# Attention slots of a decoder trunk: stick-breaking mask by GpSimd selects, fp32r carry, earlier differential combination, and two output pieces per PSUM bank

## The chip, the cores and the metric

The kernel runs on one core of a Trainium2 chip. The metric is the device time of one execution in microseconds; lower is better. The kernel before takes 606.7 us (median of three runs, 604.87 to 609.16).

Names used below: PE is TensorE (matmul), PEld its weight loads, DVE is VectorE, ACT is ScalarE, POOL is GpSimd, SP is the queue that issues most transfers.

## The reference, cut to what matters

One layer on x of 256 rows by 1024 columns, float32: a SwiGLU block, a mixer, a SwiGLU block, each followed by a residual add and a layer norm. The mixer runs three causal attentions in parallel (6 heads of 64 each) and merges them with sigmoid gates. The change touches two of them and the way the outputs of all three are stored.

```python
def stick_breaking_attention(q, k, v):
    z = jnp.einsum('bhcd,bhsd->bhcs', qc, k) * scale
    log_1m = jnp.where(before, jax.nn.log_sigmoid(-z), 0.0)      # before: key s < query t
    tail = lax.cumsum(log_1m, axis=3, reverse=True) - log_1m
    w = jnp.where(before, jnp.exp(jax.nn.log_sigmoid(z) + tail), 0.0)
    return einsum(w, v)

def diff_attention(q, k, v, slopes, lam, subln_g, lambda_init):
    p = jax.nn.softmax(s, axis=-1)            # two maps per head
    w = p[:, :, 0] - lam * p[:, :, 1]
    o = einsum(w, v)                          # then a headwise RMS norm
```

MoBA attention, with blocks as long as the sequence, is here a causal softmax with a distance bias.

## The kernel before, in words

The program is one stream per engine, written out by hand in Python; nothing reorders it (`manual_schedule`). Its backbone is weight matmuls. Every float32 weight chunk of 128 by 1024 is loaded by SP, split by ACT (high part `h`, L106) and DVE (rest `l`, L107) into two fp32r tiles, and used in three fp32r products (`nat_mm`, L381, or `trn_mm`, L389), all accumulated in PSUM tiles named `acc` (4 banks). `Weights.pump` splits ahead: each `W.done` frees a chunk and puts the next splits into ACT's and DVE's queues at that place.

The mixer walks the list `MIX` (L44): query and key projections of a pair of heads (`project`, L772), gates (`gates`, L807), branch outputs (`branch`, L829). Between them stand the attention slots. `project` queues a `slot` (L759) by `pe.later`: a model of PE's time (`Pe`, L144) runs a queued job before the matmul at which it falls due. A slot starts one new pair of heads and moves every pair under way on by one stage. So one slot is a burst of small float32 matmuls on PE, in the middle of weight matmuls, in the order of `KINDS` (L612).

There are nine pairs: three stick-breaking (S1 to S3), then three differential (D1 to D3), then three MoBA (M1 to M3), and eleven slots:

| slot | stages on PE, in order |
|---|---|
| 1 | S1 mask, S1 scores |
| 2 | S1 sums, S2 mask, S1 carry, S2 scores |
| 3 | S2 sums, S3 mask, S2 carry, S1 values, S3 scores |
| 4 | S3 sums, S3 carry, S2 values, D1 scores |
| 5 | D1 turn, S3 values, D2 scores |
| 6 | D1 pv, D2 turn, D3 scores |
| 7 | D1 turn_o, D2 pv, D3 turn, M1 scores |
| 8 | D2 turn_o, D3 pv, M1 turn, M2 scores |
| 9 | D3 turn_o, M1 values, M2 turn, M3 scores |
| 10, 11 | M2 values, M3 turn; M3 values |

Small products live in PSUM tiles `att` (4 banks of 512 columns). Per stage:

- Stick-breaking (`stick_pair`, L710). `mask` writes a mask of 0 and -1e30 into the two score banks by a matmul with the identity (`identr`, `maskr`); the scores are added on top (`start`). ACT and DVE make softplus of the scores (L726 to L729), ACT copies its high part into `ln_g` and DVE writes the rest into `ln_b` (`act_split`, L233). One slot later `sums` adds reverse cumulative sums (matmuls with the triangle `trir`), and `carry` adds the second block's total to the first by a float32 matmul with `mones`. ACT takes the exponential (L745) into tile `eT`. Another slot later `values_T` multiplies by V.
- Differential (`diff_pair`, L641). DVE adds the distance bias and finds row limits (L582), ACT exponentiates (L585). `combine` (L657) forms one map from two per head, in DVE's queue at 5.0 and 7.0 us of modelled PE time after the scores (`D_C0`, `D_C1`). A slot later `turn` transposes (ACT copies out, L593), then `pv` multiplies by V, DVE normalises out of PSUM (L680), and `turn_o` transposes the result.
- MoBA (`moba_pair`, L614). As a softmax; `norm` (L628) scales rows on DVE 4.0 us of modelled time after the scores (`M_N`), then `turn` and `values_T`.
- Storing. `values_T`, `pv` and `turn_o` take one `att` bank each. `act_split` empties that of `values_T` and `turn_o` into `oT`: ACT first (L234), DVE after it (L235); both read the bank.

Of the kernel before, what the change touches and what calls it, by code (L numbers as in the profile page):

```python
# [10 lines left out]
F32 = mybir.dt.float32  # L11
F32R = mybir.dt.float32r
AF = mybir.ActivationFunctionType
ALU = mybir.AluOpType
# [37 lines left out]
T_X1 = 5.9  # L52
T_M = 3.4
N_T = 3.0
M_N = 4.0
D_C0 = 5.0
D_C1 = 7.0
D_S = 2.5
E_BUFS = 6

# [128 lines left out]
def trunk(ctx: ExitStack, tc: tile.TileContext, start_d, x_d, ln_g, ln_b, gu_d, gun_d, down_d, v_d, qk_d, gate_d,  # L189
# [78 lines left out]

    with ExitStack() as es:
        st = es.enter_context(tc.tile_pool(name="start2", bufs=1))  # L270
        identr = const.tile([P, P], F32R, name="identr")
        nc.gpsimd.tensor_copy(identr, ident)
        mhalf = const.tile([P, 8], F32, name="mhalf")
        nc.gpsimd.memset(mhalf, -0.5)
        base = const.tile([P, BW], F32, name="base")
        iv = st.tile([P, BW], mybir.dt.int32, name="iv")
        nc.gpsimd.iota(iv[:, 0:P], pattern=[[1, P]], base=0, channel_multiplier=-1)
        nc.gpsimd.iota(iv[:, P:BW], pattern=[[1, S]], base=-P, channel_multiplier=-1)
        nc.gpsimd.tensor_copy(base, iv)
        nc.gpsimd.affine_select(base[:, 0:P], base[:, 0:P], pattern=[[-1, P]], compare_op=ALU.is_ge, fill=NEG,  # L280
                                base=0, channel_multiplier=1)
        nc.gpsimd.affine_select(base[:, P:BW], base[:, P:BW], pattern=[[-1, S]], compare_op=ALU.is_ge, fill=NEG,
                                base=P, channel_multiplier=1)
        maskf = st.tile([P, BW], F32, name="maskf")
        nc.gpsimd.memset(maskf, 0.0)
        for c in (0, S):
            nc.gpsimd.affine_select(maskf[:, c:c + P], maskf[:, c:c + P], pattern=[[1, P]], compare_op=ALU.is_gt,
                                    fill=NEG, base=0, channel_multiplier=-1)
        maskr = const.tile([P, BW], F32R, name="maskr")
        nc.gpsimd.tensor_copy(maskr, maskf)  # L290
        tri = st.tile([P, P], F32, name="tri")
        nc.gpsimd.memset(tri, -1.0)
        nc.gpsimd.affine_select(tri, tri, pattern=[[-1, P]], compare_op=ALU.is_ge, fill=0.0, base=0,
                                channel_multiplier=1)
        trir = const.tile([P, P], F32R, name="trir")
        nc.gpsimd.tensor_copy(trir, tri)
        mones = const.tile([P, P], F32, name="mones")
        nc.gpsimd.memset(mones, -1.0)
        qsc = const.tile([P, 9], F32, name="qsc")
        for b in range(3):  # L300
            for p in range(NP):
                for r in range(2):
                    h = 2 * p + r
                    v = 0.125 / SLOPES[2 * h] if b == 0 else 32.0 ** -0.5 / SLOPES[2 * h + 1] if b == 1 else 0.125
                    nc.gpsimd.memset(qsc[r * 64:(r + 1) * 64, b * NP + p:b * NP + p + 1], v)
# [221 lines left out]
    with ExitStack() as es:  # L527
# [32 lines left out]
        def scores(maps, qT, kT, row_q):  # L560


            st, mv = (qT, kT) if row_q else (kT, qT)
            first = row_q
            for kind in range(2):
                for r0, n, ps in maps:
                    r, tp = slice(r0, r0 + n), (r0, 0)
                    if row_q and kind == 0:
                        out, a, b_ = ps[:, 0:P], slice(0, P), slice(0, P)
                    elif row_q:  # L570
                        out, a, b_ = ps[:, P:BW], slice(P, S), slice(0, S)
                    elif kind == 0:
                        out, a, b_ = ps[:, 0:S], slice(0, P), slice(0, S)
                    else:
                        out, a, b_ = ps[:, S:BW], slice(P, S), slice(P, S)
                    pe.mm(out, st[r, a], mv[r, b_], first, first, tile_position=tp, share=len(maps),
                          skip_group_check=not row_q)

        def exp_rows(ps, slope, e, nmx, sm):
# [8 lines left out]
        def turn_rows(e):  # L588
# [4 lines left out]
            nc.scalar.activation(eT, ps[:, :BW], AF.Copy)  # L593
            return eT

        def values_T(b, p, eTs):

            po = att.tile([P, 512], F32, name="att")
            for kt, cs, ws in ((0, slice(0, S), slice(0, S)), (1, slice(P, S), slice(S, BW))):
                for r in range(2):  # L600
                    pe.mm(po[r * HD:(r + 1) * HD, cs], V[:, kt, vcol(b, 2 * p + r)], eTs[r][:, ws], kt == 0, kt == 1,
                          tile_position=(0, r * 64), share=2, skip_group_check=True)
            act_split(oT[b][:, p, 0:S], oT[b][:, p, S:2 * S], po[:, 0:S])
            pairs_done[b] += 1

        exps = [0]
# [2 lines left out]

        KINDS = ("sums", "mask", "carry", "turn_o", "pv", "turn", "valT", "scores")  # L612

        def moba_pair(p, qT, kT):  # L614
            sm = small.tile([P, 2, 2], F32, name="sm")
# [25 lines left out]
        def diff_pair(p, qT, kT):  # L641
# [4 lines left out]
            def start():  # L646
# [10 lines left out]
                def combine(r):  # L657
# [4 lines left out]
                    for t, cs in enumerate((slice(0, P), slice(P, BW))):  # L662
                        nc.vector.scalar_tensor_tensor(e0[:, cs], e1[:, cs], c[:, t:t + 1], e0[:, cs],  # L663
                                                       op0=ALU.mult, op1=ALU.add)
                pe.later(D_C0, lambda: combine(0))
                pe.later(D_C1, lambda: combine(1))

            def pv():
                ps = att.tile([P, 512], F32, name="att")
                for r in range(2):  # L670
                    vc, eT = vcol(1, 2 * p + r), eTs[r]
                    o0, o1 = ps[:, r * HD:(r + 1) * HD], ps[:, P + r * HD:P + (r + 1) * HD]
# [5 lines left out]
                o = ep.tile([P, S], F32, name="o", bufs=1)  # L678
                o4 = o.rearrange("p (t r c) -> p t r c", t=2, r=2)
                nc.vector.tensor_tensor(  # L680
                    o4, ps[:, 0:S].rearrange("p (t r c) -> p t r c", t=2, r=2),
                    rs.rearrange("p r t -> p t r").unsqueeze(3).to_broadcast([P, 2, 2, HD]), op=ALU.mult)
                sq = ep.tile([P, S], F32, name="s1", bufs=3)
                nc.vector.tensor_tensor(sq, o, o, op=ALU.mult)
# [11 lines left out]
                pe.later(D_S, scale)  # L696

            def turn_o():
                ps = att.tile([P, 512], F32, name="att")
                for t in range(2):  # L700
                    pe.tr(ps[:, t * P:(t + 1) * P], os_[0][:, t * P:(t + 1) * P], ident)
                act_split(oT[1][:, p, 0:S], oT[1][:, p, S:2 * S], ps[:, 0:S])
                pairs_done[1] += 1

            return [{"scores": start},
# [2 lines left out]
                    {"turn_o": turn_o}]  # L708

        def stick_pair(p, qT, kT):  # L710
            zs, sps, wts, split = [], [], [], []

            def mask():
                zs.extend(att.tile([P, 512], F32, name="att") for _ in range(2))
                for ps in zs:
                    pe.mm(ps[:, 0:BW], identr, maskr, True, False, skip_group_check=True)

            def start():
                scores([(r * 64, 64, zs[r]) for r in range(2)], qT, kT, False)
                sh = lnp.tile([P, D], F32R, name="ln_g")  # L720
                sl = lnp.tile([P, D], F32R, name="ln_b")
                split.extend((sh, sl))
                for r in range(2):
                    ps = zs[r]
                    a = ep.tile([P, BW], F32, name="e")
                    nc.scalar.activation(a, ps[:, 0:BW], AF.Abs)  # L726
                    nc.scalar.activation(a, a, AF.Exp, scale=-1.0)
                    nc.scalar.activation(a, a, AF.Ln, bias=1.0)
                    nc.vector.scalar_tensor_tensor(a, ps[:, 0:BW], 0.0, a, op0=ALU.max, op1=ALU.add)  # L729
                    sps.append(a)  # L730
                    cs = slice(r * BW, (r + 1) * BW)
                    act_split(sh[:, cs], sl[:, cs], a)

            def sums():
                for r in range(2):
                    for part in split:
                        pe.mm(zs[r][:, 0:BW], trir, part[:, r * BW:(r + 1) * BW], False, False,
                              skip_group_check=True)

            def carry():  # L740
                for r in range(2):
                    pe.mm(zs[r][:, P:S], mones, sps[r][:, S:BW], False, True, skip_group_check=True)
                for r in range(2):
                    w = ep.tile([P, BW], F32, name="eT", bufs=4)
                    nc.scalar.activation(w, zs[r][:, 0:BW], AF.Exp)  # L745
                    wts.append(w)
                exps[0] -= 1

            return [{"mask": mask, "scores": start},
                    {"sums": sums, "carry": carry},  # L750
                    {"valT": lambda: values_T(2, p, wts)}]

        attend = (moba_pair, diff_pair, stick_pair)
# [5 lines left out]
        def slot(new=None):  # L759
            if new is not None:  # L760
                under_way.append(new)
                begun[0] += 1
            now = [pair.pop(0) for pair in under_way]
            for kind in KINDS:
                for stage in now:
                    if kind in stage:
                        stage[kind]()
            under_way[:] = [pair for pair in under_way if pair]
            if begun[0] == 3 * NP and under_way:
                pe.later(PACE, slot)  # L770
# [159 lines left out]
```

## Time and profile before

| what | us |
|---|---|
| device time, median of three runs (lowest, highest) | 606.7 (604.87, 609.16) |
| the profiled execution | 606.8 |
| its span, first to last instruction | 605.1 |
| PE busy in the span | 593.8 (98%) |
| DVE, ACT, POOL busy | 407.5, 328.5, 26.9 |
| mean granted TensorE clock, of full speed | 0.995 |

The profiled execution lasted 1.7 us longer than its span; that is what lies around the first and the last instruction. The eleven slots lie between 222 and 357 us of the span. A timeline row gives start, duration, engine, line, operation, written tile, read tiles, shape and count; in square brackets stands how long the engine had been idle and what ended it. Rows merge neighbours of one kind, and a merged row lasts to the end of its last instruction. Float32 matmuls appear as two records each.

### The profile page before, as it was taken

Reading aid. Unit: us, or ns where it says so; the run is one execution under the profiler, and the core shown is the slowest. Engines: PE = TensorE matmul, PEld = TensorE weight load, DVE = VectorE, ACT = ScalarE, POOL = GpSimd, SP = SyncE. Lnnn points to the kernel's source line nnn. Section 1 sums busy time; section 2 is a strip of 40 time slices with the busy share of each in tenths; the row PEclk is TensorE's granted clock in tenths of the full one; section 3 lists DMA queues with packets and bytes.
Section 4 is the critical chain, followed back from the end, with each engine's and each line's share of the span. In section 5 each row is a group of like instructions: output and inputs, shape, how many; then the busy total and the mean of one; then the engine's idle time right before and its main releaser. Section 6 shows DMA issues by size and latency. Waiting matters only on the chain.

```text
span 605.1 us, 8603 instructions
## 1 busy us (share of the span) xinstructions
PE 593.8 (98%) x3168; PEld 506.5 (84%) x3168; DVE 407.5 (67%) x665; ACT 328.5 (54%) x561; POOL 26.9 (4%) x63
## 2 busy tenths in 40 slices
PE   8999999999999999999999999999999999999995
PEld 7888888888889988888787878888888888888884
DVE  5879767674438665577778585889857667664217
ACT  6869656653312777576556654544655655653100
POOL 1610000000001000000001000001000000000001
PEclk9999999999999999999999999999999999999998
DMA  8898755566531784444447447346965565565001
GB/s 315 289 369 307 288 181 193 186 207 202 156 104 62 249 316 166 140 147 133 144 136 221 162 140 247 117 172 228 340 194 185 185 198 173 187 192 190 1 0 70
DMA packets 32539, 113.35 MB, mean 187 GB/s; under 512 B 3681, under 2 KB 4449, under 8 KB 32497
## 3 DMA queue, kind: packets, MB, share of 16 engines
q1 hardware_dynamic: 30816, 106.97, 52.4%
q0 software_dynamic: 1680, 5.83, 2.8%
q8 instruction: 25, 0.41, 0.3%
q14 instruction: 18, 0.14, 0.1%
HBM read 111.74 MB, written 1.05 MB: 186 GB/s over the span
## 4 chain that ended last, share of the span: by engine, by line
PE 95%; DVE 2%; ACT 1%; DMA 1%; issue 1%; SPq 0%; DVEq 0%; ACTq 0%
PE acc L180 89%; PE att L180 4%; PE att L184 2%; DMA sraw<-start 1%; DVE w L107 1%; ACT e L585 1%; ACT w L106 0%; DVE e L663 0%; DVE x L356 0%; ACT eT L593 0%; SPq L244 0%; DVE x L352 0%; DVE w L235 0%; ACT w L234 0%; ACT eT L745 0%
## 5 line engine op out<-in xcount | busy, mean ns | idle before, releaser
L107 DVE TENSOR_TENSOR w<-raw,w 128x1024 fp32r<-128x1024 f32 (+1 forms) x166 | 197.6, 1206 | 75.1 <-ACT w L106 74.9
L180 PE MATMUL acc<-xT,w 128*128 128x512 f32 x1264 | 225.3, 338 | 0.0
L180 PEld LDWEIGHTS acc<-xT,w 128*128 128x128 f32 x1264 | 193.6, 188 | 28.6 <-issue 1.0
L106 ACT ACTIVATE w<-raw 128x1024 fp32r<-128x1024 f32 (+1 forms) x166 | 170.3, 1041 | 80.0 <-PE acc L180 66.4
L180 PE MATMUL acc<-w,xT 128*128 128x512 f32 (+1 forms) x576 | 129.2, 379 | 0.0
L180 PEld LDWEIGHTS acc<-w,xT 128*128 128x128 f32 x576 | 105.2, 188 | 18.0 <-issue 1.0
L180 PE MATMUL acc<-w,hT 128*128 128x512 f32 (+1 forms) x408 | 93.5, 383 | 0.0
L180 PEld LDWEIGHTS acc<-w,hT 128*128 128x128 f32 x408 | 74.9, 188 | 14.9
L459 ACT ACTIVATE lo<-acc 128x256 f32<-128x256 f32 x76 | 27.8, 375 | 58.2 <-PE acc L180 58.2
L461 DVE TENSOR_TENSOR gu<-acc,lo 128x256 f32<-128x256 f32 x76 | 31.2, 419 | 38.6 <-ACT lo L459 38.6
L107 DVE TENSOR_TENSOR wx<-raw,wx 128x1024 fp32r<-128x1024 f32 (+1 forms) x30 | 36.3, 1212 | 12.0 <-ACT wx L106 12.0
L180 PE MATMUL acc<-xT,wx 128*128 128x512 f32 x240 | 44.0, 338 | 0.0
L180 PEld LDWEIGHTS acc<-xT,wx 128*128 128x128 f32 x240 | 36.7, 188 | 5.4
L106 ACT ACTIVATE wx<-raw 128x1024 fp32r<-128x1024 f32 (+1 forms) x30 | 31.3, 1046 | 10.9 <-PE acc L180 10.4
L180 PE MATMUL acc<-wx,hT 128*128 128x512 f32 (+1 forms) x138 | 32.8, 380 | 0.0
L180 PEld LDWEIGHTS acc<-wx,hT 128*128 128x128 f32 x138 | 25.2, 188 | 4.9
L338 DVE SCALAR_TENSOR_TENSOR x<-x,acc 128x512 f32<-128x512 f32 x11 | 7.5, 682 | 28.0 <-PE acc L180 28.0
L180 PE MATMUL acc<-w,oT 128*128 128x512 f32 x108 | 26.0, 394 | 0.0
L347 POOL TENSOR_TENSOR rs<-rs,mhalf 128x1 f32<-128x1 f32 x6 | 5.9, 979 | 408.0 <-DVE rs L346 408.0
L234 ACT ACTIVATE hT<-gu 128x256 fp32r<-128x256 f32 x40 | 16.6, 415 | 13.1 <-DVE gu L466 12.1
L180 PEld LDWEIGHTS acc<-w,oT 128*128 128x128 f32 x108 | 20.0, 188 | 4.4 <-issue 0.3
L465 ACT ACTIVATE gu<-gu 128x256 f32<-128x256 f32 x40 | 16.4, 409 | 2.8 <-DVE gu L461 2.6
(135 smaller groups left out, 401.4 us busy)
## 6 DMA issues: line engine op xcount, KB each, us to landing
raw<-gu SPq DMA_DIRECT2D x76, 512.0 KB, 4.9
raw<-down SPq DMA_DIRECT2D x44, 512.0 KB, 4.1
raw<-gates SPq DMA_DIRECT2D x24, 512.0 KB, 4.4
raw<-qk SPq DMA_DIRECT2D x18, 512.0 KB, 4.5
raw<-v SPq DMA_DIRECT2D x12, 384.0 KB, 3.1
raw<-w_out SPq DMA_DIRECT2D x8, 512.0 KB, 4.3
raw<-gun SPq DMA_DIRECT2D x8, 512.0 KB, 4.6
sraw<-start SPq DMA_DIRECT2D x7, 384.0 KB, 6.4
```

The source lines that it names most:

```text
L106: self.nc.scalar.activation(h[:, :n], raw[:, :n], AF.Copy)
L107: self.nc.vector.tensor_tensor(l[:, :n], raw[:, :n], hv[:, :n], op=ALU.subtract)
L180: self.nc.tensor.matmul(out, lhsT=lhsT, rhs=rhs, start=start, stop=stop, **kw)
L184: self.nc.tensor.transpose(out, in_, ident)
L234: nc.scalar.activation(dst_h, src, AF.Copy)
L338: nc.vector.scalar_tensor_tensor(xs, xs, ALPHA, ps[:, 0:n], op0=ALU.mult, op1=ALU.add)
L347: nc.gpsimd.tensor_tensor(rs, rs, mhalf[:, 0:1], op=ALU.pow)
L459: nc.scalar.activation(lo, ps[:, S:2 * S], AF.Copy)
L461: nc.vector.tensor_tensor(v, ps[:, 0:S], lo, op=ALU.add)
L465: nc.scalar.activation(g, g, AF.Silu)
L585: nc.scalar.activation(e[:, cs], e[:, cs], AF.Exp, bias=nmx[:, t:t + 1], scale=-1.0, accum_out=sm[:, t:t + 1])
```

## The change

Four edits, all inside the slots:

1. The mask matmuls go. The first score matmul now opens the accumulation, and GpSimd zeroes the future with `affine_select` twice per head: on the softplus tile before it is split (`unseen(a)`), and on the exponential (`unseen(w)`).
2. The carry is done in fp32r, on the two parts (`ln_g`, `ln_b`) that the sums use, right after each head's sums; it was one float32 matmul per head. Each head's exponential follows its own carry.
3. `combine` of a differential pair is queued at once, behind its exponentials, and `M_N` falls from 4.0 to 2.0.
4. `half_bank` hands out halves of an `att` bank: within one slot the first two of `turn_o`, `pv` and `values_T` share a bank.

```diff
-M_N = 4.0
-D_C0 = 5.0
-D_C1 = 7.0
+M_N = 2.0
...
-        mones = const.tile([P, P], F32, name="mones")
+        mones = st.tile([P, P], F32, name="mones")
         nc.gpsimd.memset(mones, -1.0)
+        monesr = const.tile([P, P], F32R, name="monesr")
+        nc.gpsimd.tensor_copy(monesr, mones)
...
-                    pe.mm(out, st[r, a], mv[r, b_], first, first, tile_position=tp, share=len(maps),
+                    pe.mm(out, st[r, a], mv[r, b_], row_q or kind == 0, row_q, tile_position=tp, share=len(maps),
...
+        halves = []
+
+        def half_bank():
+
+            if not halves:
+                ps = att.tile([P, 512], F32, name="att")
+                halves.extend((ps[:, 0:S], ps[:, S:2 * S]))
+            return halves.pop(0)
+
         def values_T(b, p, eTs):
 
-            po = att.tile([P, 512], F32, name="att")
+            po = half_bank()
...
-        KINDS = ("sums", "mask", "carry", "turn_o", "pv", "turn", "valT", "scores")
+        KINDS = ("sums", "turn_o", "pv", "turn", "valT", "scores")
...
-                pe.later(D_C0, lambda: combine(0))
-                pe.later(D_C1, lambda: combine(1))
+                for r in range(2):
+                    combine(r)
 
             def pv():
-                ps = att.tile([P, 512], F32, name="att")
+                ps = half_bank()
...
             def turn_o():
-                ps = att.tile([P, 512], F32, name="att")
+                ps = half_bank()
...
-            def mask():
+            def unseen(a):
+
+                blocks = a.rearrange("p (n c) -> p n c", c=P)[:, 0:3:2, :]
+                nc.gpsimd.affine_select(blocks, blocks, pattern=[[0, 2], [1, P]], compare_op=ALU.is_gt, fill=0.0,
+                                        base=0, channel_multiplier=-1)
+
+            def start():
                 zs.extend(att.tile([P, 512], F32, name="att") for _ in range(2))
-                for ps in zs:
-                    pe.mm(ps[:, 0:BW], identr, maskr, True, False, skip_group_check=True)
-
-            def start():
...
-                    sps.append(a)
+                    unseen(a)
                     cs = slice(r * BW, (r + 1) * BW)
                     act_split(sh[:, cs], sl[:, cs], a)
...
-
-            def carry():
-                for r in range(2):
-                    pe.mm(zs[r][:, P:S], mones, sps[r][:, S:BW], False, True, skip_group_check=True)
-                for r in range(2):
+                    for n, part in enumerate(split):
+                        pe.mm(zs[r][:, P:S], monesr, part[:, r * BW + S:(r + 1) * BW], False, n == 1,
+                              skip_group_check=True)
                     w = ep.tile([P, BW], F32, name="eT", bufs=4)
                     nc.scalar.activation(w, zs[r][:, 0:BW], AF.Exp)
+                    unseen(w)
                     wts.append(w)
...
             now = [pair.pop(0) for pair in under_way]
+            halves.clear()
```

Three places show what moves. The first is PE in slot 7, with buffer numbers and the engines waited for. `ident,o` are the transposes of `turn_o` for D1, `V,eT` the matmuls of `pv` for D2, `ident,e` the transposes of `turn` for D3. Before:

```order
L184 MATMUL att_3066<-ident_117,o_2895 128x128 x2
L180 MATMUL att_3071<-V_1930,eT_2907 128x64 [waits Activation_49]
L180 MATMUL att_3071<-V_1930,eT_2907 128x64 x2
L180 MATMUL att_3071<-V_1930,eT_2913 128x64 x3
L184 MATMUL att_3088<-ident_117,e_2927 128x128 x3
```

and now:

```order
L182 MATMUL att_3068<-ident_117,o_2897 128x128 [waits Activation_49]
L182 MATMUL att_3068<-ident_117,o_2897 128x128
L178 MATMUL att_3068<-V_1920,eT_2909 128x64 [waits DVE_49]
L178 MATMUL att_3068<-V_1920,eT_2909 128x64 x2
L178 MATMUL att_3068<-V_1920,eT_2915 128x64 [waits Activation_49]
L178 MATMUL att_3068<-V_1920,eT_2915 128x64 x2
L182 MATMUL att_3089<-ident_117,e_2929 128x128 [waits PE_49]
```

`turn_o` and `pv` wrote two banks (att_3066, att_3071) and now write one (att_3068). The first matmul of `pv` waited for an ACT copy of the slot before and now waits for DVE: for the subtraction by which `act_split` empties the half that `turn_o` wrote. Slot 8 has the same rows, and in slot 9 the first `values_T` matmul of M1 waits so for D3's `turn_o`.

The second place is the row of DVE in which D2's maps are combined, from the last row limits of slot 5 on. `qT` and `kT` empty a projection, `w<-raw,w` are weight splits, the rows with `c` are `combine`. Before:

```order
L787 SCALAR_TENSOR_TENSOR qT<-acc,qsc,s_2812 128x256
L790 TENSOR_TENSOR kT<-acc,s_2833 128x256
L107 TENSOR_TENSOR w<-raw,w 128x1024 x2
L659 RECIPROCAL c<-smd 128x2
L660 SCALAR_TENSOR_TENSOR c<-smd,nlam,c 128x2
L663 SCALAR_TENSOR_TENSOR e<-e,c 128x128
L663 SCALAR_TENSOR_TENSOR e<-e,c 128x256
L107 TENSOR_TENSOR w<-raw,w 128x1024
L659 RECIPROCAL c<-smd 128x2
L660 SCALAR_TENSOR_TENSOR c<-smd,nlam,c 128x2
L663 SCALAR_TENSOR_TENSOR e<-e,c 128x128
L663 SCALAR_TENSOR_TENSOR e<-e,c 128x256
```

and now:

```order
L658 RECIPROCAL c<-smd 128x2
L659 SCALAR_TENSOR_TENSOR c<-smd,nlam,c 128x2
L662 SCALAR_TENSOR_TENSOR e<-e,c 128x128
L662 SCALAR_TENSOR_TENSOR e<-e,c 128x256
L658 RECIPROCAL c<-smd 128x2
L659 SCALAR_TENSOR_TENSOR c<-smd,nlam,c 128x2
L662 SCALAR_TENSOR_TENSOR e<-e,c 128x128
L662 SCALAR_TENSOR_TENSOR e<-e,c 128x256
L788 SCALAR_TENSOR_TENSOR qT<-acc,qsc,s_2824 128x256
L791 TENSOR_TENSOR kT<-acc,s_2845 128x256
L105 TENSOR_TENSOR w<-raw,w 128x1024 x3
```

Both combinations moved ahead of the projection's emptying and of three weight splits.

The third place is POOL from the first norm's powers to the end of the stick-breaking pairs; `e` is the softplus tile, `eT` the exponential, `bg` the gate bias. Now:

```order
L338 TENSOR_TENSOR rs<-rs,mhalf 128x1 x2
L715 AFFINE_SELECT e<-e 128x2x128 x2
L812 DMA bg<-b_gate 128x1024 x2
L715 AFFINE_SELECT eT<-eT 128x2x128 x2
L715 AFFINE_SELECT e<-e 128x2x128 x2
L715 AFFINE_SELECT eT<-eT 128x2x128 x2
L715 AFFINE_SELECT e<-e 128x2x128 x2
L715 AFFINE_SELECT eT<-eT 128x2x128 x2
```

Before, only the two powers and the two transfers of `bg` stood there; twelve selects are added, two of them ahead of `bg`.

## Rows read from the trace of the kernel before

**Rows 1.** The chain that ended last, by engine (page, part 4).
```profile
PE 95%; DVE 2%; ACT 1%; DMA 1%; issue 1%; SPq 0%; DVEq 0%; ACTq 0%
```
**Rows 2.** Waits of PE inside the mixer: line waited for, us in total, times, longest.
```profile
PE att L184 <- DVE e L663: 0.9, 1, 0.9
PE att L180 <- ACT eT L593: 0.5, 2, 0.3
PE att L180 <- ACT eT L745: 0.4, 1, 0.4
```
**Rows 3.** Timeline, PE in slot 2: mask, carry, scores.
```profile
234.03 0.51 PE L180 MATMUL att<-maskr,identr 128*128 128x384 f32 x2
...
234.38 0.61 PE L180 MATMUL att<-e,mones 128*128 128x128 f32 x4
...
234.92 0.92 PE L180 MATMUL att<-qT,kT 64*128 64x256 f32 x8
```
**Rows 4.** Timeline, PEld in slot 7: pv, six float32 matmuls of 64 columns.
```profile
306.60 1.42 PEld L180 LDWEIGHTS att<-V,eT 128*128 128x128 f32 x12
```
**Rows 5.** Timeline, POOL's selects at the start, and DVE beside them.
```profile
14.88 5.24 DVE L107 TENSOR_TENSOR w<-raw,w 128x1024 fp32r<-128x1024 f32 x4 [0.71 <-ACT w L106]
...
17.66 1.37 POOL L282 TENSOR_SCALAR_AFFINE_SELECT base<-base 128x256 f32<-128x256 f32 x1
...
21.30 0.29 POOL L293 TENSOR_SCALAR_AFFINE_SELECT tri<-tri 128x128 f32<-128x128 f32 x1
```
**Rows 6.** Timeline, S3: end of its split, and its first sum in slot 4.
```profile
257.48 0.56 DVE L235 TENSOR_TENSOR ln_b<-e,ln_g 128x384 fp32r<-128x384 f32 x1 [0.59 <-ACT ln_g L234]
...
260.02 0.35 PE L180 MATMUL att<-ln_g,trir 128*128 128x384 f32 x1
```
**Rows 7.** Gate bias: first use (timeline); its transfers, us to landing (page, part 6).
```profile
244.53 1.28 DVE L825 TENSOR_TENSOR G<-acc,bg 128x512 f32<-128x512 f32 x2
...
bg<-b_gate POOLq DMA_DIRECT2D x3, 512.0 KB, 8.4
```
**Rows 8.** Timeline, PEld in slots 6 and 5: turn, and what follows it.
```profile
289.72 0.37 PEld L184 LDWEIGHTS att<-ident,e 128*128 128x128 f32 x3
...
291.96 0.19 PEld L180 LDWEIGHTS acc<-kT,qT 32*128 32x128 f32 x2 [0.17 <-issue]
...
277.06 0.79 PEld L184 LDWEIGHTS att<-ident,e 128*128 128x128 f32 x6
...
278.02 0.63 PEld L180 LDWEIGHTS att<-eT,V 128*64 128x64 f32 x8 [0.17 <-issue]
```
**Rows 9.** Timeline, slot 7: pv on PE; DVE up to emptying turn_o's bank.
```profile
306.71 1.45 PE L180 MATMUL att<-V,eT 128*128 128x64 f32 x12
306.82 2.36 DVE L107 TENSOR_TENSOR w<-raw,w 128x1024 fp32r<-128x1024 f32 x2 [0.52 <-ACT w L106]
...
309.10 0.42 DVE L235 TENSOR_TENSOR oT<-att,oT 128x256 fp32r<-128x256 f32 x1
```
**Rows 10.** Timeline, slot 8: the same, with the MoBA scaling (L633) on DVE.
```profile
316.32 2.36 DVE L107 TENSOR_TENSOR w<-raw,w 128x1024 fp32r<-128x1024 f32 x2 [0.52 <-ACT w L106]
...
318.27 1.45 PE L180 MATMUL att<-V,eT 128*128 128x64 f32 x12
...
318.80 1.01 DVE L633 TENSOR_SCALAR e<-e,rsm 128x128 f32<-128x128 f32 x4
...
320.12 0.41 DVE L235 TENSOR_TENSOR oT<-att,oT 128x256 fp32r<-128x256 f32 x1
```
**Rows 11.** Timeline, slot 9: M1's values on PE; DVE empties turn_o's bank, then M1's.
```profile
330.86 0.87 PE L180 MATMUL att<-eT,V 128*64 128x256 f32 x8
...
332.09 0.75 DVE L235 TENSOR_TENSOR oT<-att,oT 128x256 fp32r<-128x256 f32 x2
```
**Rows 12.** Windows at the end: us, PE, PEld, DVE, ACT, POOL busy (x), PEclk, DMA, GB/s.
```profile
597.50:598.00 0.50, 0.26 (x3) 0.06 (x1) 0.20 (x1) 0.00 (x0) 0.00 (x0) 1.00 0.00 0
...
599.50:600.00 0.50, 0.00 (x0) 0.00 (x0) 0.50 (x2) 0.00 (x0) 0.50 (x1) 0.63 0.00 0
```

More of the change, by code (lines that the diff above doesn't have):

```diff
@@ L270, in trunk @@
         st = es.enter_context(tc.tile_pool(name="start2", bufs=1))
-        identr = const.tile([P, P], F32R, name="identr")
-        nc.gpsimd.tensor_copy(identr, ident)
         mhalf = const.tile([P, 8], F32, name="mhalf")
@@ L283, in trunk @@
                                 base=P, channel_multiplier=1)
[L284 to L290, printed above, removed]
         tri = st.tile([P, P], F32, name="tri")
@@ L563, in scores @@
             st, mv = (qT, kT) if row_q else (kT, qT)
-            first = row_q
             for kind in range(2):
@@ L602, in values_T @@
                           tile_position=(0, r * 64), share=2, skip_group_check=True)
-            act_split(oT[b][:, p, 0:S], oT[b][:, p, S:2 * S], po[:, 0:S])
+            act_split(oT[b][:, p, 0:S], oT[b][:, p, S:2 * S], po)
             pairs_done[b] += 1
@@ L680, in pv @@
                 nc.vector.tensor_tensor(
-                    o4, ps[:, 0:S].rearrange("p (t r c) -> p t r c", t=2, r=2),
+                    o4, ps.rearrange("p (t r c) -> p t r c", t=2, r=2),
                     rs.rearrange("p r t -> p t r").unsqueeze(3).to_broadcast([P, 2, 2, HD]), op=ALU.mult)
@@ L698, in turn_o @@
             def turn_o():
-                ps = att.tile([P, 512], F32, name="att")
+                ps = half_bank()
                 for t in range(2):
                     pe.tr(ps[:, t * P:(t + 1) * P], os_[0][:, t * P:(t + 1) * P], ident)
-                act_split(oT[1][:, p, 0:S], oT[1][:, p, S:2 * S], ps[:, 0:S])
+                act_split(oT[1][:, p, 0:S], oT[1][:, p, S:2 * S], ps)
                 pairs_done[1] += 1
@@ L710, in stick_pair @@
         def stick_pair(p, qT, kT):
-            zs, sps, wts, split = [], [], [], []
-            def mask():
+            zs, wts, split = [], [], []
+            def unseen(a):
[3 more added lines that the diff above has]
+            def start():
                 zs.extend(att.tile([P, 512], F32, name="att") for _ in range(2))
-                for ps in zs:
-                    pe.mm(ps[:, 0:BW], identr, maskr, True, False, skip_group_check=True)
-            def start():
                 scores([(r * 64, 64, zs[r]) for r in range(2)], qT, kT, False)
@@ L738, in sums @@
                               skip_group_check=True)
-            def carry():
-                for r in range(2):
-                    pe.mm(zs[r][:, P:S], mones, sps[r][:, S:BW], False, True, skip_group_check=True)
-                for r in range(2):
+                    for n, part in enumerate(split):
+                        pe.mm(zs[r][:, P:S], monesr, part[:, r * BW + S:(r + 1) * BW], False, n == 1,
+                              skip_group_check=True)
                     w = ep.tile([P, BW], F32, name="eT", bufs=4)
                     nc.scalar.activation(w, zs[r][:, 0:BW], AF.Exp)
+                    unseen(w)
                     wts.append(w)
                 exps[0] -= 1
-            return [{"mask": mask, "scores": start},
-                    {"sums": sums, "carry": carry},
+            return [{"scores": start},
+                    {"sums": sums},
                     {"valT": lambda: values_T(2, p, wts)}]
```

## Prediction, written before the changed kernel was run

> **What bounds the kernel now.** I read the chain of waits first. 95% of the span lies on PE, 1% each on ACT and on transfers and 2% on DVE [rows 1]. So an edit pays only by the PE time it takes out or the PE waits it ends, and it costs what it puts on PE, work or wait. Then I read the waits of PE inside the mixer: four, 1.8 us in all [rows 2]. One is for the combination (DVE, L663, slot 6), two are for an ACT copy of transposed rows (L593, slots 7 and 8), one is for an exponential (L745, slot 3). All four are waits for an operand or for an `att` bank, and the change goes for all of them. Last I read the timeline of the slots for what DVE and ACT do while PE is in a slot. There the change adds three waits, so most of the working below is about them.
>
> **Mask and carry on PE.** In slot 2 the mask matmuls start at 234.03, the carry at 234.38, the scores at 234.92 [rows 3]. So the mask takes 0.35 us of PE and the carry 0.54 us, per pair. Three masks go: 3 x 0.35 = 1.05 us gained. The carry becomes four fp32r matmuls of 128 columns per pair. No fp32r matmul that narrow is in the trace. The nearest row is `pv`, whose twelve records are narrower still (64 columns) and take 1.42 us, 0.118 us each [rows 4]: at that size the record, not its columns, sets the time. I take 4 x 0.118 = 0.47 us, a gain of 3 x (0.54 - 0.47) = 0.2 us. The two ends: if only columns counted, a third of the mask's 0.175 us, 0.058 us each, the gain is 3 x (0.54 - 0.23) = 0.9 us; if narrow fp32r ran no faster than a carry matmul of before, 0.54 / 2 = 0.27 us each, there is a loss of 3 x (1.08 - 0.54) = 1.6 us.
>
> **Selects on GpSimd.** Twelve, of 256 elements per partition each. At the start a select of 128 took 0.29 us while DVE's splits were over, and one of 256 took 1.37 us while four of them ran [rows 5]. I take 0.4 us, since the select on the softplus follows DVE's own last step and DVE's next one waits for the split behind it; the ends are 0.3 and 1.4. A new wait comes with it: ACT's copy of the high part now waits for POOL, and behind it in ACT's queue stand the next head's softplus, the copies of a projection and weight splits. That is about 0.9 us more per pair. The tightest pair is S3: its split ends at 257.48 + 0.56 = 258.04 and the first sum starts at 260.02 [rows 6], a cover of 1.98 us. So it is hidden, and at 1.4 us (2.8 in all) up to 0.8 us shows. PE waits nowhere in the mixer for a weight split [rows 2], so splits 0.9 us late cost nothing as long as that cover lasts. The selects on the exponentials have a whole slot until the values read them. The `bg` transfers move behind S1's first selects, so at the latest to slot 2, by when S1's split must be done: 234 us [rows 3]. Landing takes 8.4 us and the first use is at 244.53 [rows 7], so 2 us at least are left over: nothing.
>
> The Trainium skill (SBUF — State Buffer, "SBUF: two separate sides") says that GpSimd and a DVE instruction with two SBUF inputs lock each other out of a shared port pair for a whole instruction. The two selects of rows 5 fit it: 1.37 us beside such splits. By that rule a select costs at most one split more, which is the upper end already taken, and the sum stays as it is.
>
> **The exponential's bank (slot 3).** S1's values waited 0.4 us for a bank that S2's first exponential had to free [rows 2]. Without the early masks the values take a bank free since slot 2, and each exponential starts half a stage earlier. Gain 0.4 us.
>
> **Combination at once (slot 6).** Transposes took 289.72 to 291.96 there, 2.24 us; the same six took 277.06 to 278.02, 0.96 us, in slot 5, where nothing was waited for [rows 8]. Queued behind the exponentials, the maps are ready before slot 6 begins, so 1.28 us go. Late next is the bank that D3's scores take over from `pv`: DVE can normalise as soon as `pv` ends, while PE transposes, so nothing follows. The price is that DVE waits for ACT's eight exponentials with a projection's emptying and splits behind it. PE waits for none of these in the mixer [rows 2], so I count nothing; without that cover, the 1.28 us come back.
>
> **Two pieces per bank.** In slots 7 and 8 the scores waited twice, 0.5 us in all, for a bank that an ACT copy had to free [rows 2]; one bank less per slot ends that: gain 0.5 us. But the second piece now waits until DVE has emptied the first, and DVE has weight splits ahead of that. PE stands in order, so everything behind the first matmul of the second piece waits too: `pv`, `turn`, the scores, then the weight matmuls.
> - Slot 7: `pv` started at 306.71. DVE splits two chunks from 306.82 to 309.18, then empties `turn_o` from 309.10 to 309.52 [rows 9]. These follow the projection's end as before, and the combination moved away stood ahead of them. Loss 309.52 - 306.71 = 2.81 us.
> - Slot 8: `pv` started at 318.27, the emptying at 320.12. The smaller `M_N` takes the scaling, 1.01 us, out of DVE's way, to a place ahead of the splits that end at 318.68 [rows 10]. So 320.12 - 1.01 + 0.41 = 319.52. Loss 1.25 us; 2.26 us if the scaling were still in the way.
> - Slot 9: M1's values started at 330.86; DVE begins the two emptyings at 332.09 behind a split [rows 11], and the first ends 0.42 us later (its length in rows 9). Loss 332.51 - 330.86 = 1.65 us.
>
> Together 5.7 us. A piece alone in its bank (slots 3 to 6, 10, 11) pays nothing.
>
> The Trainium skill (PSUM — Partial Sum Buffer, "PSUM bank collisions raise a hardware error") says that TensorE must not write a bank in the partitions where another engine reads it, even in other columns. So halves of one bank can't be filled and emptied at once, and the wait is none that a finer bookkeeping of columns could drop; without the rule the 5.7 us would be 0. No run here shows the collision itself.
>
> **The sum.** Gains: 1.05 + 0.2 + 0.4 + 1.28 + 0.5 = 3.4 us. Losses: 5.7 us. Net 2.3 us more. The profiled execution took 606.8 us (605.1 span, 1.7 around it), 0.1 over the median, so I forecast 606.8 + 2.3 = 609.1 us, 0.4% slower. About 1%, 6 us, is what a measurement of this kernel can tell from no change, so this counts as the same. Its own range is 607 to 611.5: carry from +0.7 to -1.8 around my term, 1.0 us more in slot 8, 0.8 us for slow selects, 1 us less if ACT and DVE reach the emptying sooner.
>
> **Rivals.**
> - The gains alone: the three half-bank waits are short, because DVE comes to the emptying as soon as ACT has copied. The row of DVE speaks against it: two splits in slot 7, one in slot 9 stand ahead in program order, and each must wait for ACT. For it speaks only that splits have moved elsewhere on DVE. It decides if the three waits together are under 3.4 us. Time 606.8 - 3.4 = 603.4 us, faster. Chance 0.14.
> - The clock falls in slot 7. PE ended at about 597.8; the granted clock was 1.00 for nearly two us more, then in the window from 599.5 it was 0.63 on the way to the lower of its two levels, 1.2 GHz [rows 12]. A stop of 2.8 us in slot 7 is longer than that. Against it: no stop inside the mixer was over 0.9 us [rows 2], so no row shows a fall between bursts, nor how long a low stretch lasts. Each us at the lower level loses half a us. If it takes as long to rise as it took to fall, 1 us is lost; if it lasts to slot 8, 11 us on, 5.5 us. I take 1.5: 610.6 us, up to 614.6. Chance 0.25.
> - The selects are slow, 1.4 us each, and the carry as slow as before per matmul: 0.8 + 1.8 us more, 611.7 us. Speaking for it: the only select of that width took 1.37 us. Against: DVE is idle in that step. Chance 0.08.
>
> The Trainium skill (TensorE: Matmul & The Clock Gate, "Why this matters for your kernels") warns of idle gaps between bursts of matmuls, since the clock goes back to its lower level. The end of this trace agrees that it does.
>
> **How the numbers follow.** Forecast 0.53, gains alone 0.14, clock 0.25, slow selects and carry 0.08. The likeliest gives 609.1. The range takes in the gains alone at 603.4 and ends at 612.5, which leaves out the upper tail of the clock case. Faster by over 1% (under 600.7) would need all gains and more: 0.02. Slower by over 1% (over 612.8) is that tail and a little of the last case: 0.07. Within 1%: 0.91.
>
> **What would show it.** Right: three new waits of PE for DVE's emptying of `oT`, near 2.8, 1.25 and 1.65 us, the only long ones in the mixer; slot 6 without a wait for the combination; no row of `maskr`; narrow carry records near 0.12 us; selects near 0.4 us and no PE wait for `ln_g` or `ln_b`; granted clock 1.00 through slots 7 to 9. Wrong: PE waits under 3.4 us in all there (faster), a granted clock below 1.00 behind slot 7, or PE waiting for POOL or for a weight split (slower).

## The result, and the profile after

The changed kernel takes 610.3 us (median of 22 executions, 606.59 to 613.38), the kernel before, run beside it, 606.88 (22 executions). The ratio is 1.0052, with 95% interval 1.0037 to 1.0067: 3.2 us slower (2.2 to 4.1). The forecast was 2.3 us slower, 609.1.

The execution that was profiled took 606.59 us, the fastest of the 22, and 0.2 us less than the profiled one of before. So this trace alone doesn't show the loss. Rows of its chain of waits and of that of before show why: where the long run of weight matmuls starts, what follows slot 11, and the last block. Before:

```profile
17.86 168.10 PE acc L180 x892
...
356.99 27.92 PE acc L180 x122
...
439.29 158.49 PE acc L180 x839
```

and now:

```profile
18.23 168.10 PE acc L178 x892
...
358.57 27.92 PE acc L178 x122
...
440.93 156.63 PE acc L178 x839
```

The slots end 1.6 us later, but the last block, which no edit touches, takes 1.86 us less; the last section comes back to it. What else is lacking, the clock, comes with the second and third profile below.

The page of the changed kernel, parts 1 and 4 (busy time; the chain that ended last):

```profile
PE 590.0 (98%) x3162; PEld 504.4 (83%) x3162; DVE 407.1 (67%) x665; ACT 327.6 (54%) x561; POOL 33.5 (6%) x71
...
PE 89%; DMA 3%; issue 3%; DVE 3%; ACT 1%; POOL 0%; SPq 0%; DVEq 0%; ACTq 0%; POOLq 0%
```

PE is busy for 590.0 us, where it was 593.8; 1.86 of these 3.8 us are the last block. PE's share of the chain was 95% [rows 1]. It is smaller now mostly because the chain passes over DVE, POOL and transfers ahead of the last block; that costs nothing, since from slot 11 to the last block the two traces take 82.36 and 82.30 us. The waits of PE (line waited for, us in total, times, longest):

```profile
PE att L178 <- DVE oT L233: 5.4, 3, 2.7
```

None of the four waits of [rows 2] is left. In their place stand three for DVE's emptying of `oT`, 5.4 us, as forecast. The timeline, in order of time: the split of S1, slot 2, the split of S3 and its first sum, slots 7, 8 and 9.

```profile
225.88 0.41 POOL L715 TENSOR_SCALAR_AFFINE_SELECT e<-e 128x256 f32<-128x256 f32 x1 [32.31 <-DVE e L730]
...
233.57 0.35 PE L178 MATMUL att<-ln_g,trir 128*128 128x384 f32 x1
...
233.93 0.22 PE L178 MATMUL att<-ln_g,monesr 128*128 128x128 f32 x1
...
234.77 0.92 PE L178 MATMUL att<-qT,kT 64*128 64x256 f32 x8
235.05 1.79 POOL L715 TENSOR_SCALAR_AFFINE_SELECT eT<-eT 128x256 f32<-128x256 f32 x2 [4.42 <-ACT eT L744]
...
257.24 0.56 DVE L233 TENSOR_TENSOR ln_b<-e,ln_g 128x384 fp32r<-128x384 f32 x1 [1.07 <-ACT ln_g L232]
...
259.30 0.35 PE L178 MATMUL att<-ln_g,trir 128*128 128x384 f32 x1
...
303.84 0.38 PE L182 MATMUL att<-ident,o 128*128 128x128 f32 x2
304.17 2.36 DVE L105 TENSOR_TENSOR w<-raw,w 128x1024 fp32r<-128x1024 f32 x2 [0.52 <-ACT w L104]
306.45 0.42 DVE L233 TENSOR_TENSOR oT<-att,oT 128x256 fp32r<-128x256 f32 x1
306.92 1.55 PE L178 MATMUL att<-V,eT 128*128 128x64 f32 x12 [2.70 <-DVE oT L233]
309.06 0.93 PE L178 MATMUL att<-kT,qT 64*128 64x128 f32 x8
317.66 0.38 PE L182 MATMUL att<-ident,o 128*128 128x128 f32 x2
...
319.07 1.55 PE L178 MATMUL att<-V,eT 128*128 128x64 f32 x12 [1.03 <-DVE oT L233]
...
321.21 0.93 PE L178 MATMUL att<-kT,qT 64*128 64x128 f32 x8
...
330.10 0.38 PE L182 MATMUL att<-ident,o 128*128 128x128 f32 x2
...
332.77 0.87 PE L178 MATMUL att<-eT,V 128*64 128x256 f32 x8 [1.64 <-DVE oT L233]
333.57 0.93 PE L178 MATMUL att<-kT,qT 64*128 64x128 f32 x8
```

The rows of slot 7 answer to [rows 9]: DVE does the same two splits and the emptying, and `pv` now waits behind them. Between `turn_o` and the matmul that follows it in the same bank lie 3.08, 1.41 and 2.67 us, where the trace of before has 0.22, 0.22 and 0.97 (in slot 9 other transposes stand between). `turn_o` in the trace of before, for [rows 9], [rows 10] and [rows 11]:

```profile
306.49 0.38 PE L184 MATMUL att<-ident,o 128*128 128x128 f32 x2
...
318.05 0.38 PE L184 MATMUL att<-ident,o 128*128 128x128 f32 x2
...
329.89 0.38 PE L184 MATMUL att<-ident,o 128*128 128x128 f32 x2
```

So the shared banks cost 2.86 + 1.19 + 1.70 = 5.75 us (forecast 2.81 + 1.25 + 1.65 = 5.71).

**An account of the slots.** `turn_o` of slot 7 starts at 303.84; before, at 306.49. Since the long run of weight matmuls starts 0.37 us later in this trace (18.23 against 17.86), the edits 1 to 3 have given 3.0 us by then. From there to the last values of slot 11 (ending at 358.57 and 356.99) the changed kernel loses 4.2 us. Of these, 5.75 are the shared banks; 1.57 come back from the MoBA scores (last row of each slot): 0.93 us each now, where they took 1.30, 1.30 and 1.26, with 0.25 of idle time ahead of two of them. Their rows in the trace of before:

```profile
309.07 1.30 PE L180 MATMUL att<-kT,qT 64*128 64x128 f32 x8 [0.25 <-ACT eT L593]
...
320.63 1.30 PE L180 MATMUL att<-kT,qT 64*128 64x128 f32 x8 [0.25 <-ACT eT L593]
...
331.66 1.26 PE L180 MATMUL att<-kT,qT 64*128 64x128 f32 x8
```

Together -3.0 + 5.75 - 1.57 = +1.2 us. What lies between that and the +3.2 of the measurement is the clock, as the next profiles show.

### The profile page after: what moved, and what is told of

It is laid out like the page before. It is cut to its first block, busy times and chain, and to the rows that moved or that the text cites. A ratio compares the mean times of both kernels' runs of the same rounds, so it can differ in the third digit from the quotient of the medians.

```text
span 604.9 us, 8601 instructions
## 1 busy us (share of the span) xinstructions
PE 590.0 (98%) x3162; PEld 504.4 (83%) x3162; DVE 407.1 (67%) x665; ACT 327.6 (54%) x561; POOL 33.5 (6%) x71
## 4 chain that ended last, share of the span: by engine, by line
PE 89%; DMA 3%; issue 3%; DVE 3%; ACT 1%; POOL 0%; SPq 0%; DVEq 0%; ACTq 0%; POOLq 0%
PE acc L178 83%; PE att L178 4%; DMA raw<-gu 2%; PE att L182 1%; DMA sraw<-start 1%; ACT w L104 1%; DVE wx L105 1%; DVE w L105 1%; POOL rs L338 0%; DVE x L347 0%; DVE x L343 0%; SPq L242 0%; ACT wx L104 0%; DVE oT L233 0%; ACT s L790 0%
```

## Experiments

For every kernel below, the mean granted clock is the mean over all its executions, of which each lists its own; the kernel before lies at 0.9963, 0.9968 and 0.9969 in three groups of runs, 0.9967 over all. The mean takes in the end of an execution, where PE has finished and the clock is low [rows 12]: the profiled executions of before and of the change both list 0.995, with 1.00 up to there. So the mean of one execution doesn't show a fall behind a stop; a difference between means over many executions does, as far as their ends are alike. "Slots" is the account above, made anew from that kernel's trace. Read in one piece instead, from the chain's row of 148 matmuls ahead of slot 1 to the end of slot 11, less what the low clock took in that profile, it comes out within 0.4 us of these sums.

**Whole banks again.** Only edit 4 is undone.

```diff
-            if not halves:
-                ps = att.tile([P, 512], F32, name="att")
-                halves.extend((ps[:, 0:S], ps[:, S:2 * S]))
-            return halves.pop(0)
+            return att.tile([P, 512], F32, name="att")[:, 0:S]
```

> The changed kernel with edit 4 undone: every piece has a bank of its own again. Theory (PE stands until DVE has emptied the first half): no wait of PE for DVE's oT is left, so the 5.4 us that the changed kernel's profile shows for them come back, less 0.5 us for the two ACT waits of slots 7 and 8 that return: 610.3 - 5.4 + 0.5 = 605.4 us, 1.5 us under the kernel before (606.9) or lower. Rival (GpSimd's selects, or the longer ACT queue behind them, are what costs): stays at 609 to 611 us.

Measured 603.28 us, ratio 0.992 (0.9888 to 0.9952): 4.9 us below the kernel before. Mean clock 0.9967. The waits for `oT` are gone; one of the two for transposed rows is left:

```profile
PE att L178 <- ACT eT L583: 0.3, 1, 0.3
```

So edits 1 to 3 are a gain, and edit 4 alone makes the change slower.

**Shared banks alone.** The kernel before with edit 4 (`half_bank` in `values_T`, `pv` and `turn_o`, and `halves.clear()` in the slot).

> The kernel before with edit 4 alone. Theory: three waits of PE for DVE's oT, 2.8 us in slot 7, 2.2 us in slot 8 (the scaling still stands ahead of the emptying there) and 1.65 us in slot 9, less the 0.5 us of the two ACT waits: 606.9 + 6.1 = 613.0 us. Rival (the waits are cheap alone and the selects cost): within 1 us of 606.9.

Measured 617.44 us, ratio 1.0163 (1.0127 to 1.0198): 9.9 us slower. That is more than the 6.1 us expected, and more than its three waits for `oT` (6.5 us) can be. The windows of its trace show why (length, busy time of PE, PEld, DVE, ACT, POOL, granted clock, DMA share, GB/s):

```profile
307.00:309.00 2.00, 0.00 (x0) 0.00 (x0) 2.00 (x3) 0.82 (x2) 0.00 (x0) 1.00 0.07 20
309.00:311.00 2.00, 1.61 (x13) 1.61 (x14) 0.42 (x2) 0.00 (x0) 0.00 (x0) 0.91 0.95 332
311.00:313.00 2.00, 2.00 (x13) 1.67 (x14) 1.44 (x4) 0.98 (x2) 0.24 (x1) 0.50 0.42 170
313.00:315.00 2.00, 2.00 (x12) 1.25 (x11) 1.00 (x7) 0.67 (x3) 0.78 (x1) 0.74 0.01 2
...
325.00:327.00 2.00, 2.00 (x11) 2.00 (x11) 0.00 (x0) 0.00 (x0) 0.00 (x0) 0.50 0.44 176
```

PE stands still through the first window. Then it works again, and only then the granted clock falls, to its lower level of 1.2 GHz: 0.91, 0.50 and 0.74 lose 2 x (0.09 + 0.50 + 0.26) = 1.7 us of matmul. The second fall, in the windows from 323 on, follows a stop of 2.2 us in slot 8 and loses 3.4 us. The mean clock is 0.9887; against 0.9963 that is 0.0076 x 615 = 4.7 us. Slots: 2.86 + 2.33 + 1.70 - 1.57 = +5.3. Sum +10.0.

**The changed kernel, profiled twice more.** No edit; the first:

> The changed kernel once more, for another profiled execution. Theory with the clock: either the granted clock stays at 1.00 behind slot 7 and the time is 606 to 608 us, or it drops to 0.50 for some us there and the time is 609 us or more. Without the clock: no drop in any execution, whatever the time.

It took 609.64 us. The second:

> As the run before, for a third profiled execution of the changed kernel.

It took 611.37 us. Both have the three waits of 5.4 us in all. The windows around the stop in slot 7, which begins at 304 to 306 us, in the profile of 606.59 us:

```profile
305.00:307.00 2.00, 0.08 (x1) 0.09 (x1) 1.95 (x4) 0.35 (x2) 0.00 (x0) 1.00 0.33 98
...
309.00:311.00 2.00, 2.00 (x16) 1.52 (x15) 1.93 (x10) 1.36 (x5) 0.87 (x1) 1.00 0.34 135
```

in that of 609.64 us:

```profile
307.00:309.00 2.00, 2.00 (x17) 1.78 (x16) 0.72 (x2) 0.42 (x1) 0.00 (x0) 0.85 0.90 266
309.00:311.00 2.00, 2.00 (x10) 1.24 (x10) 0.92 (x4) 0.56 (x2) 1.01 (x1) 0.50 0.39 158
311.00:313.00 2.00, 2.00 (x10) 1.77 (x10) 1.34 (x9) 1.86 (x8) 0.00 (x0) 0.80 0.00 0
```

and in that of 611.37 us:

```profile
309.00:311.00 2.00, 2.00 (x12) 2.00 (x12) 0.46 (x2) 0.00 (x0) 0.00 (x0) 0.52 0.87 277
311.00:313.00 2.00, 2.00 (x12) 1.28 (x10) 0.98 (x3) 0.98 (x2) 0.87 (x1) 0.50 0.23 92
313.00:315.00 2.00, 2.00 (x8) 1.55 (x7) 1.54 (x9) 1.30 (x7) 0.14 (x1) 0.50 0.00 0
315.00:317.00 2.00, 2.00 (x10) 1.73 (x10) 0.16 (x1) 1.03 (x4) 0.00 (x0) 0.78 0.00 0
```

The same program after the same stop of 2.70 us loses nothing, 1.7 us or 3.4 us. Over its 22 executions the mean clock is 0.9934; against 0.9967 that is 0.0033 x 609 = 2.0 us. With the slots, +1.2 + 2.0 = +3.2 us, as measured.

**Sharing everywhere but in slot 7, and sharing in slot 7 only.** Both count slots; the first takes a whole bank `if n_slot[0] == 7`, the second `if n_slot[0] != 7`.

```diff
+        n_slot = [0]
...
+            if n_slot[0] == 7:
+                return att.tile([P, 512], F32, name="att")[:, 0:S]
             if not halves:
                 ps = att.tile([P, 512], F32, name="att")
...
             halves.clear()
+            n_slot[0] += 1
```

> The changed kernel with banks of their own in slot 7 alone; slots 8 and 9 still share. Theory with the clock (the changed kernel's stop of 2.7 us in slot 7 brings the granted clock down in many executions, as it did in the profile of edit 4 alone): over the kernel with whole banks (603.3) only the waits of slots 8 and 9 remain, 1.03 + 1.64 = 2.7 us, too short for a fall: 606 us, clock 1.00 throughout. Without the clock (the rest of the changed kernel's 7.0 us over whole banks is a cost of sharing in all three slots): 607.5 to 608.5 us.

> The changed kernel with banks of their own everywhere but in slot 7. Theory with the clock: 603.3 + 2.7 for the wait, less 0.25 for the ACT wait there, plus 1.5 to 2 us where the clock falls: 606 to 608 us, by execution one or the other. Without the clock: 605.7 us, and no wider spread than the others.

Without sharing in slot 7: 607.35 us, ratio 1.0002 (0.9973 to 1.003), mean clock 0.9967 (0.9968 before). That is 1.3 us above the 606 expected, though the interval, -1.6 to +1.8 us, holds it (slots: -1.1). Sharing in slot 7 only: 608.18 us, 1.0009 (0.9988 to 1.003), mean clock 0.9934, 2.1 us lost; slots -1.4, sum +0.7, measured +0.5. By their times alone the two can't be told apart. The clock tells them apart: 16 of the 22 executions of the change and 9 of the 12 with sharing in slot 7 only list 0.994 or less, and none of the 12 without sharing in slot 7. So the falls come with the stop of 2.7 us, and not with those of 1.0 and 1.6. One thing stands beside that: 6 of the 77 listed executions of the kernel before also lie at 0.993 or 0.994, and take 609.6 us on average where the others take 607.0. None of the six has a profile, so whether the clock can fall between bursts without a long stop stays open.

**Edits 1 and 2 alone, and edit 3 alone.** Both on whole banks: the first with the constants and queueing of `combine` of before, the second with the mask and carry of before.

> The kernel before with edits 1 and 2 alone (mask by selects, carry in fp32r). Theory: 1.05 us for three masks, 0.15 us for three carries (0.49 us instead of 0.54 us each in the changed kernel's profile) and 0.4 us for the wait of slot 3: 606.9 - 1.6 = 605.3 us, and no wait of PE for a weight split. Rival (selects cost): 607 to 610 us.

> The kernel before with edit 3 alone (combination queued at once, M_N 2.0). Theory: the wait of slot 6 goes, 1.28 us: 605.6 us, and the emptyings in slots 7 to 9 don't matter, since nobody waits for them. Rival (DVE blocked behind the exponentials delays splits that PE needs): 607 us or more.

Edits 1 and 2: 605.54 us, 0.9981 (0.996 to 1.0001), slots -1.6. Edit 3: 605.23 us, 0.9981 (0.9957 to 1.0004), slots -1.9 (1.28 of slot 6, and the scores of slot 8, 0.62). Both lie 1.2 us below before, and each interval just reaches no change, so neither gain is shown by itself; the two together are, by the kernel with whole banks. In the first the combination in slot 6 is waited for as before, in the second the exponential in slot 3:

```profile
PE att L184 <- DVE e L661: 0.9, 1, 0.9
```

```profile
PE att L178 <- ACT eT L743: 0.4, 1, 0.4
```

**Work between the two pieces of a bank.** The changed kernel, with another order in the slot; the second run moves the transposes only.

```diff
-        KINDS = ("sums", "turn_o", "pv", "turn", "valT", "scores")
+        KINDS = ("sums", "turn_o", "turn", "scores", "pv", "valT")
```

> The changed kernel with the order of stages sums, turn_o, turn, scores, pv, valT: banks are still shared, but the transposes and the scores of other pairs stand between the two pieces of a bank. If the loss is that PE stands idle in order, and not the sharing itself, the waits for the emptying shrink by what is put between (0.75 us of transposes and 0.85 of scores in slots 7 and 8, 0.85 in slot 9, where transposes stood between already): 2.7 to 1.1, 1.0 to 0, 1.6 to 0.8, 1.9 us left of 5.4. Then no stop is as long as 2.2 us, the granted clock stays at 1.00 from 303 to 345 us, and its mean over the executions is that of the kernel before (0.9967). Time 607.0 - 3.0 - 1.6 + 1.9 = 604.3 us; up to 1.1 us more if the scores wait for banks. If sharing costs by itself, 607 us or more.

> The changed kernel with the order sums, turn_o, turn, pv, valT, scores: only the transposes stand between the two pieces of a bank. Waits for the emptying 2.7 to 1.95 and 1.0 to 0.3 us, the third unchanged at 1.6; 3.9 us in all, and the scores again wait for a bank that an ACT copy frees (0.25 us of idle and 0.35 of stretched matmuls per slot). Time about 607 to 608 us. The clock is open: the stop in slot 7 lies between one of 1.6 us, behind which it never fell, and one of 2.2, behind which it did.

With transposes and scores between: 605.17 us, 0.9953 (0.9932 to 0.9974), 2.9 us below before; mean clock 0.9969, as before. Its waits:

```profile
PE att L178 <- ACT eT L583: 0.8, 2, 0.5
...
PE att L178 <- DVE oT L233: 0.2, 1, 0.2
```

Sharing a bank costs little by itself; what costs is PE standing behind it in order. With the transposes alone between (`"sums", "turn_o", "turn", "pv", "valT", "scores"`):

```profile
PE att L178 <- DVE oT L233: 4.1, 3, 2.0
```

608.97 us, 1.0022 (0.9994 to 1.0049), 1 us above what was expected. Slots: -0.1. The mean clock is 0.9946 against 0.9969, 1.4 us: behind the stop of 2.0 us in slot 7 the clock must fall in some executions; the profiled one shows 1.00 there, so this rests on the listed clocks alone. They fall into two groups: seven of the 12 executions at 0.992 or 0.993, with 610.0 us on average, and five at 0.996 to 0.998, with 606.7.

**Transposes ahead of all, on whole banks, and whole banks once more.**

```diff
-        KINDS = ("sums", "turn_o", "pv", "turn", "valT", "scores")
+        KINDS = ("sums", "turn", "turn_o", "pv", "valT", "scores")
```

> Whole banks (edit 4 undone) and the order sums, turn, turn_o, pv, valT, scores, so that ACT's copies of transposed rows are done when the scores want their banks. In the whole-bank kernel the scores of slots 7 and 9 took 1.30 and 1.26 us against 0.93 where their second bank was free in time, and 0.25 us of idle stood ahead of one. If that stretch is a wait for ACT inside the burst, all three take 0.93 us, 1.0 us less in all: 1.0 us below the whole-bank kernel run beside it. If 1.30 us is something else, the same time.

> The whole-bank kernel once more, on the same chip as the three others: 602 to 604 us, 4 to 5 us below the kernel before, and its mean clock over the executions is that of the kernel before.

602.29 us, 0.9908 (0.9881 to 0.9936), 5.6 us below before; whole banks again 605.18, 0.9949 (0.9924 to 0.9973), 3.1 below, which misses the 602 to 604 expected. The MoBA scores of slot 7, first here and then in the kernel with whole banks:

```profile
307.20 0.93 PE L178 MATMUL att<-kT,qT 64*128 64x128 f32 x8
```

```profile
308.12 1.30 PE L178 MATMUL att<-kT,qT 64*128 64x128 f32 x8 [0.25 <-ACT eT L583]
```

In slot 9 they take 0.99 against 1.26. So the longer burst is a wait for ACT's copy inside the burst, where its second map takes over a bank. The two kernels differ by 2.9 us, where 1.0 was expected, and the traces account for 0.9 (0.25 + 0.37 + 0.27); the intervals overlap, and the blocks outside the slots vary by as much as the rest (last section). This version has the lowest median of all, though it isn't shown to be faster than whole banks: it keeps edits 1 to 3, leaves out edit 4, and ends the waits that edit 4 was there to end.

The two accounts beside each other, in us against the kernel before:

| kernel | slots | clock | sum | measured (95%) |
|---|---|---|---|---|
| shared banks alone | +5.3 | +4.7 | +10.0 | +9.9 (7.7, 12.0) |
| the change | +1.2 | +2.0 | +3.2 | +3.2 (2.2, 4.1) |
| transposes between | -0.1 | +1.4 | +1.3 | +1.3 (-0.4, 3.0) |
| sharing in slot 7 only | -1.4 | +2.1 | +0.7 | +0.5 (-0.7, 1.8) |
| sharing everywhere but in slot 7 | -1.1 | +0.1 | -1.0 | +0.1 (-1.6, 1.8) |
| edits 1 and 2 alone | -1.6 | -0.2 | -1.8 | -1.2 (-2.4, 0.1) |
| edit 3 alone | -1.9 | -0.4 | -2.3 | -1.2 (-2.6, 0.2) |
| scores between | -2.2 | 0.0 | -2.2 | -2.9 (-4.1, -1.6) |
| whole banks, first and again | -3.6 | -0.2 | -3.8 | -4.9 (-6.8, -2.9), -3.1 (-4.6, -1.6) |
| transposes ahead, whole banks | -4.6 | +0.2 | -4.4 | -5.6 (-7.2, -3.9) |

Every sum lies in the interval beside it. Up to 0.4 us in the clock column can be the ends of the executions, and several sums miss the middle of the interval by up to 1.2 us. So the account of the change is right to about 1 us, and that it meets the measured 3.2 to a tenth is luck.

## Why the prediction was right, and by which errors

The time lies in the forecast's own range, 607 to 611.5, but the sum behind it came out by two errors of opposite sign: a gain that was 1.1 us too small, and the clock, put at nothing in the sum, which cost 2.0. That they cancel in part is luck. The measured +3.2 lies nearer to the clock rival's +3.8 than to the forecast's +2.3, and one of the prediction's own signs of being wrong, a clock below 1.00 behind slot 7, was seen. It also held a change under 1% for the same; the 22 executions of each kernel tell 3.2 us from none.

- **Mask and carry.** Right. From S1's first sum to the first score pass 1.20 us. Two sums take 0.36 (233.57 to 233.93), four 0.72, which leaves 0.48 for the carry (forecast 0.47); the mask's 0.35 are gone.
- **Selects on GpSimd.** 0.41 us with DVE at rest (taken: 0.4). Beside weight splits two take 1.79, one of them 0.40 and the other 1.43, as the row of the start, 1.37, suggested; there nobody waits for them. (The prediction set one split more equal to its upper end, 1.4; 0.4 and a split of 1.2 make 1.6.) S3's split ends at 257.80 and its sum starts at 259.30: 1.5 us of cover left, and no wait of PE for it.
- **Slots 3 and 6.** Both waits are gone. `pv` of slot 6, before and now:

```profile
288.54 1.45 PE L180 MATMUL att<-V,eT 128*128 128x64 f32 x12
```

```profile
287.29 1.45 PE L178 MATMUL att<-V,eT 128*128 128x64 f32 x12
```

With the 0.37 us of the start, 1.62 us are gained by then (forecast for masks, carries and slot 3: 1.65), and another 1.40 from there to `turn_o` of slot 7 (forecast for slot 6: 1.28).

- **The half-bank waits.** Right: the three losses to 0.06 us each, the idle time in them to 0.3. The reason given holds: the splits ahead in DVE's queue, and in slot 8 the scaling out of the way (with it in the way, in the kernel with shared banks alone, slot 8 loses 2.33 us; forecast 2.26). "The gains alone" falls with that: the three waits are 5.4 us, not under 3.4.
- **The waits for ACT in slots 7 and 8.** The step that failed in the sum: "gain 0.5 us". It counted the idle time of [rows 2]. The second map waited inside the burst as well, in slot 9 too, and that stood in the profile as busy PE. The gain is 1.57 us: 2 x 0.25 idle, and 0.37 + 0.37 + 0.33 of stretched matmuls. With it the slots come to +1.2 us, where the sum had 2.3.
- **The clock.** The rival with chance 0.25 happened, though not in every execution: two of three profiles show it, and the mean over all is 2.0 us (taken: 1.5, with 1 and 5.5 as bounds). At half the clock, 1.7 and 3.4 us lost are 3.4 and 6.8 us at the lower level. What spoke against it, that no stop inside the mixer was over 0.9 us, only meant that the trace had not met the case. The Trainium skill (TensorE: Matmul & The Clock Gate, "Why this matters for your kernels") warns of idle gaps between bursts of matmuls; the windows above agree, inside the kernel as at its end, though not in every execution.

So 2.3 had the right sign and some 70% of the size, with a wrong split: it was 1.2 from the slots and 2.0 from the clock. Slow selects with a slow carry, 0.08, did not happen.

## What to carry to other kernels

Two pieces that share a bank are one resource: what fills the second waits for the last reader of the first, with all that stands ahead of that reader in its own queue, so put other work of PE between them, or the sharing costs more than it saves; even with such work between, it was not faster here than a bank for each piece. A stop of PE must be priced twice: for its length, and for the lower clock that can follow (here behind stops of 2.2 and 2.7 us, and by the listed clocks 2.0). And look for a wait inside a burst: compare the length of equal bursts where one has its banks in time, since busy time hides it.

## What was not expected of the hardware

- The granted clock fell after stops of PE of 2.2 and 2.7 us, and by the listed clocks of 2.0, in some executions and not in others. Behind these stops the traces show it falling only once PE was working again: windows within the stop read 1.00, and 0.50 to 0.91 stands in those behind it. At the kernel's end, where PE does not start again, it fell while PE stood [rows 12]. A fall took 1.7 or 3.4 us of work in the traces, whether after 2.7 or 2.2 us. Behind stops of 1.0 and 1.6 us no trace shows one. What decides between none, one and the longer one stays open.
- Outside the slots one program varies too: the last block's matmuls in the chain of waits take 156.63 us in some executions and 158.48 in others, of kernels that are the same there, both at full clock. The first block's take 168.10 or 170.24, in the same way. Against the changed kernel's rows in the section on the result (156.63 and 168.10) stand, below, those of its profile at 609.64 us, and of the kernel without sharing in slot 7. Together that is 4.0 us from one execution to another, more than the change costs. Its cause stays open.

```profile
442.12 158.48 PE acc L178 x839
```

```profile
17.75 170.24 PE acc L178 x892
```
